# A two-block transformer in float32: new orders in the first stage, attention in head pairs, and the position products moved behind other projections

## The chip, the cores and the metric

One core of a Trainium2 chip runs the whole program. The time is device microseconds of one execution. TensorE is called PE here, VectorE DVE, ScalarE ACT, and SyncE SP; SP issues the loads.

## The reference, cut to what matters

256 tokens of width 2048 run through two blocks in float32.

```python
# first block: x, ctx are [256, 2048]
mod = silu(c) @ w_ada + b_ada                     # also for c_ctx; six vectors of 2048
h   = rms_norm(x) * (1 + sc_a) + sh_a             # the same for ctx with its own vectors
qa, kva, kr, cb, cc, ch = split(h @ w_in)         # ctx gives keys and values only
s   = q_nope @ k_nope.T + q_rope @ k_rope.T       # 8 heads: 128 + 64 wide, 256 + 256 keys
att = softmax(s / sqrt(192)) @ v
x   = x + gt_a * (rms_norm_by_group(concat(att, conv)) @ w_out)
x   = rms_norm(x + gt_f * conv_ffn(modulate(rms_norm(x))))       # 5504 wide
# second block, layers i = 0 (sparse attention) and 1 (stick-breaking attention)
x = layer_norm(ALPHA * x + (o * silu(gate)) @ w_o, g, b)
x = x + (p[i] @ w_ple[i]) * sigmoid(x @ w_ple_gate[i])           # p[i] is [256, 256]
```

## The kernel before, in words

Activations lie feature-major: a tile [128, k, 256] holds 128 features of block k for 256 tokens. A weight matrix comes in raw chunks of up to 1 MB on SP's queue into 4 slots (`issue`, L338). A unit of 1024 columns of a chunk is split in two: ACT casts a high part wh (L357), DVE subtracts for the low part wl (L358). A product is three matmuls of 256 columns, wh·xh, wl·xh, wh·xl (`mm3`), all recorded at L409. Splits run 4 units ahead of the matmuls (`look`, `unit`), with 5 buffers, and a chunk's slot is loaded anew when its last unit is split.

Tables fix the order. FIRST gives the matmul order of the first stage: `a` is a w_ada quarter, whose chunk PE takes raw, c and q the first columns of the short convolution and the query, k the keys and values. LOADS gives the order of their loads. LATE says after which chunk of a later weight a "late" block of w_ada follows, 64 in all: these are reduced on DVE, one instruction of 2048 columns each (L347), in the same queue as the splits. Work off the main product runs as generators in three lanes (EV, SIDE, MISC), which `pump` steps once after a unit.

First stage: four transposes give CBC; `gen_r0` sums the squares of x (w = 0) or ctx (w = 1) and multiplies by a matrix of ones; after each four `a`, `gen_h` writes SHG (shift and scale) and X, XH, XL for two blocks. Then come the short convolution's group 1, kv norm, the key and value products (wkvk, wkvv), the queries (wqb) with rope on KR and QR, and the rest of the convolution, between whose units `gen_att` runs one head and 128 queries at a time, up to four at once (ATT = (4, 2)).

w_out's first two groups end together (`turns`); then `resid` takes groups: it adds into x (`upd`, for w_out `upd_out`), squares, sums, and ends with matmuls with ones. PSUM has a ring of 2 tiles with 2 banks each (MR) and one of 4 banks (SR), so w_out's third group starts when `upd_out` has read the first.

At the end of each layer `finish_layer` runs w_o through `resid`, the four groups of p @ w_ple, the layer norm (`gen_ln`, `pair`), and the gate product. p arrives as PF, split in PH and PL.

## Time and profile before

| | us |
|---|---|
| three runs | 2202.58, 2196.92, 2197.62 (median 2197.62) |
| the profiled execution, its own time | 2194.55 |
| its span | 2192.7 |
| PE busy | 2148.4 (98%) |
| DVE busy | 1494.7 (68%) |
| ACT busy | 1104.9 (50%) |

Times in the rows are in the span's microseconds. In a timeline a row has its start, its duration (from the first start to the last end for a row with xN), the engine, the line, the operation, out<-in with shapes, and in brackets how long the engine was idle before it and who released it. In the list of waits "A <- B" says that A's engine waited for B. PEclk is the clock granted to PE, 1.00 being 2.4 GHz and 0.50 being 1.2 GHz. A matmul on 32-bit data that are not split (ones, scores) shows as two records.

### The profile page before, as it was taken

The numbers are of one execution on the slowest core, as the hardware profiler recorded it, in microseconds if no ns is written. First come the engines' busy times: TensorE is split into PE (matmuls) and PEld (weight loads), VectorE is DVE, ScalarE is ACT, GpSimd is POOL, SyncE is SP. The second block draws the span as 40 slices with busy tenths as digits, with TensorE's granted clock in tenths as the row PEclk, the third lists the DMA queues.
The fourth block names the chain that finished last, engine by engine and source line by source line (L and its number), as shares of the span: only waits on it lengthen the run. The fifth ranks groups of instructions, "written<-read, shape, count | busy, mean of one in ns | idle before, by whom it ended". The sixth has DMA issues, their size and how long they took to land.

```text
span 2192.7 us, 40082 instructions
## 1 busy us (share of the span) xinstructions
PE 2148.4 (98%) x17272; PEld 2058.8 (94%) x17272; DVE 1494.7 (68%) x1992; ACT 1104.9 (50%) x1512; POOL 0.2 (0%) x4
## 2 busy tenths in 40 slices
PE   5999999999999999999999999999999999999999
PEld 3779789989999999999999999999999999999999
DVE  4457878878767676757877669666666746646575
ACT  4345455445544444445656443445446546645363
POOL 0000000000000000000000000000000000000000
PEclk9999999999999999999999999999999999999999
DMA  9874878867666666645555544444555554455553
GB/s 395 335 278 175 324 260 308 344 242 288 230 223 239 231 233 236 223 176 190 187 187 187 186 164 177 150 154 154 197 174 181 188 192 142 147 173 190 181 176 113
DMA packets 68434, 467.71 MB, mean 213 GB/s; under 512 B 7840, under 2 KB 8352, under 8 KB 16544
## 3 DMA queue, kind: packets, MB, share of 16 engines
q1 hardware_dynamic: 68256, 465.14, 58.6%
q8 instruction: 135, 2.21, 0.4%
q14 instruction: 43, 0.35, 0.0%
HBM read 463.01 MB, written 2.10 MB: 212 GB/s over the span
## 4 chain that ended last, share of the span: by engine, by line
PE 94%; DMA 2%; DVE 2%; ACT 1%; issue 0%; SPq 0%; DVEq 0%; ACTq 0%
PE m L409 80%; PE s L409 14%; DMA raw<-in_wada 1%; DMA rawx<-in_wqa 1%; PE s L406 1%; DVE wl L358 1%; ACT wh L357 0%; DMA X<-in_xt 0%; DVE sq L616 0%; DVE raw L347 0%; DVE rp L1285 0%; DVE rp L1286 0%; DVE X L1144 0%; ACT uf L1204 0%; DVE uf L1212 0%
## 5 line engine op out<-in xcount | busy, mean ns | idle before, releaser
L409 PE MATMUL m<-XH,wh 128*128 128x256 f32 x4032 | 1144.8, 284 | 5.8 <-ACT XH L1185 4.1
L358 DVE TENSOR_TENSOR wl<-raw,wh 128x1024 fp32r<-128x1024 f32 (+1 forms) x672 | 800.2, 1197 | 502.9 <-ACT wh L357 501.6
L409 PE MATMUL m<-XH,wl 128*128 128x256 f32 x4032 | 1133.2, 281 | 2.9 <-DVE wl L358 2.9
L409 PE MATMUL m<-XL,wh 128*128 128x256 f32 x4032 | 1133.2, 281 | 0.3 <-DVE XL L1188 0.3
L357 ACT CAST wh<-raw 128x1024 fp32r<-128x1024 f32 (+1 forms) x672 | 687.0, 1029 | 665.8 <-PE m L409 587.4
L409 PEld LDWEIGHTS m<-XH,wh 128*128 128x128 f32 x4032 | 762.7, 189 | 27.6 <-issue 20.7
L409 PEld LDWEIGHTS m<-XH,wl 128*128 128x128 f32 x4032 | 762.5, 189 | 6.4 <-DVE wl L358 3.3
L409 PEld LDWEIGHTS m<-XL,wh 128*128 128x128 f32 x4032 | 762.2, 189 | 0.7 <-DVE XL L1188 0.6
L409 PE MATMUL m<-ahl,wh 128*128 128x256 f32 x1376 | 245.0, 281 | 0.5 <-DVE uf L1213 0.5
L409 PEld LDWEIGHTS m<-ahl,wh 128*128 128x128 f32 x1376 | 211.3, 188 | 0.7 <-issue 0.7
L409 PE MATMUL m<-ahl,wl 128*128 128x256 f32 x688 | 193.1, 281 | 0.0
L347 DVE SCALAR_TENSOR_TENSOR raw<-raw,CBC 128x2048 f32<-128x2048 f32 x64 | 145.0, 2283 | 0.0
L409 PEld LDWEIGHTS m<-ahl,wl 128*128 128x128 f32 x688 | 129.7, 189 | 0.0
L409 PE MATMUL s<-XH,wh 128*128 128x256 f32 x416 | 117.9, 283 | 7.1 <-ACT XH L649 7.1
L409 PE MATMUL s<-XL,wh 128*128 128x256 f32 x416 | 117.9, 283 | 0.0
L409 PE MATMUL s<-XH,wl 128*128 128x256 f32 x416 | 117.6, 283 | 0.0
L362 ACT CAST ahl<-AC 128x512 fp32r<-128x512 f32 x88 | 53.7, 610 | 89.0 <-PE m L409 89.0
L409 PEld LDWEIGHTS s<-XH,wh 128*128 128x128 f32 x416 | 79.4, 191 | 7.3 <-ACT XH L649 7.3
L363 DVE TENSOR_TENSOR ahl<-AC,ahl 128x512 fp32r<-128x512 f32 x88 | 59.6, 677 | 38.5 <-ACT ahl L362 38.5
L409 PEld LDWEIGHTS s<-XH,wl 128*128 128x128 f32 x416 | 79.4, 191 | 0.0
L409 PEld LDWEIGHTS s<-XL,wh 128*128 128x128 f32 x416 | 79.4, 191 | 0.0
L358 DVE TENSOR_TENSOR wl<-rawx,wh 128x768 fp32r<-128x768 f32 (+1 forms) x24 | 25.0, 1046 | 60.7 <-ACT wh L357 60.7
(387 smaller groups left out, 1683.4 us busy)
## 6 DMA issues: line engine op xcount, KB each, us to landing
raw<-in_wada SPq DMA_DIRECT2D x96, 1024.0 KB, 7.0
raw<-in_wup SPq DMA_DIRECT2D x86, 1024.0 KB, 4.9
raw<-in_wdown SPq DMA_DIRECT2D x40, 1024.0 KB, 4.8
raw<-in_wpg SPq DMA_DIRECT2D x32, 1024.0 KB, 4.9
raw<-in_wconv SPq DMA_DIRECT2D x28, 768.0 KB, 5.6
raw<-in_wout SPq DMA_DIRECT2D x16, 1024.0 KB, 6.4
raw<-in_wqA SPq DMA_DIRECT2D x16, 1024.0 KB, 4.8
raw<-in_wgA SPq DMA_DIRECT2D x16, 1024.0 KB, 4.8
```

The costliest lines, as they stand in the source:

```text
L347: V.scalar_tensor_tensor(r, r, 1.0, CBC, op0=OP.mult, op1=OP.mult, accum_out=ADA[:, b:b + 1])
L357: S.copy(e.wh[:, :n], r)
L358: V.tensor_tensor(e.wl[:, :n], r, e.wh[:, :n].bitcast(F32), OP.subtract)
L362: S.copy(e.x[:, 0, :e.nk], a)
L363: V.tensor_tensor(e.x[:, 1, :e.nk], a, e.x[:, 0, :e.nk].bitcast(F32), OP.subtract)
L406: count[0] = TE.transpose(o, i, ident)
L409: count[0] = TE.matmul(ps, l, r, start=start, stop=stop, skip_group_check=True, **kw)
```

## The change

1. LOADS: C0 moves between the second and third `a`; in the steady part each Q goes behind the two `a` that it preceded. After every fourth `a`, `look(1)` becomes `look(0)`. CBC is copied by DVE, not ACT. The sums for x are started before the first `a`, their ones matmul comes behind the second; those for ctx run at one go behind c1, with 8 matmuls with ones in place of most of the adds.
2. LATE: the convolution gets 24 blocks instead of 30, wkvv 1 and wqb 5 that had none.
3. `gen_att` takes two heads at a time, two such pairs at once (ATT = (2, 4)); the two 64-row products stand side by side, one on rows 0 to 63, the other on rows 64 to 127.
4. The layers' output projections end in two halves of 256 columns, as w_out did. In `resid` the sums of the first half go into `acc` on DVE, and only the last two blocks are summed by matmuls at the end. `ones` holds 1/2048 from w_out on.
5. Of the 8 groups of p @ w_ple, 2 go behind w_out, 3 behind the first w_o and 3 behind the second (before: 0, 4, 4). Early results are parked in DRAM (stored on ACT's queue, loaded on SP's). `parts`, which loads pf and splits it, now stands ahead of `resid`.

The rows in the following lists are in program order of one engine.

PE at the first scores, before (KN, QN: 128-wide part; KR, QR: 64-wide part):

```order
1049 L409 MATMUL m<-XL,wh 128x256
1050 L409 MATMUL s<-KN,QN 128x512
1051 L409 MATMUL s<-KR,QR 128x512
1052 L409 MATMUL m<-XH,wh 128x256
1053 L409 MATMUL m<-XH,wl 128x256
1054 L409 MATMUL m<-XL,wh 128x256
```

PE at the same place, after:

```order
1052 L415 MATMUL m<-XL,wh 128x256
1053 L415 MATMUL s<-KN,QN 128x512 x2
1054 L415 MATMUL s<-KR,QR 128x512 x2
1055 L415 MATMUL m<-XH,wh 128x256
1056 L415 MATMUL m<-XH,wl 128x256
1057 L415 MATMUL m<-XL,wh 128x256
```

Two heads' 128-wide products now stand together, and then their two 64-wide ones.

DVE in the middle of w_out, before (gta: the gate vector; X<-m,gta,X: `upd_out`; raw,ADA: a late block):

```order
310 L347 SCALAR_TENSOR_TENSOR raw,ADA<-raw,CBC 128x2048 x2
311 L358 TENSOR_TENSOR wl<-raw,wh 128x1024 x4
312 L1141 TENSOR_TENSOR gta<-ADA,vecs 128x16
313 L1144 SCALAR_TENSOR_TENSOR X<-m,gta,X 128x256 x4
314 L347 SCALAR_TENSOR_TENSOR raw,ADA<-raw,CBC 128x2048 x2
315 L358 TENSOR_TENSOR wl<-raw,wh 128x1024
316 L1144 SCALAR_TENSOR_TENSOR X<-m,gta,X 128x256 x4
```

DVE at the same place, after (ph<-pf,ph: the subtraction in `parts`):

```order
291 L353 SCALAR_TENSOR_TENSOR raw,ADA<-raw,CBC 128x2048 x2
292 L364 TENSOR_TENSOR wl<-raw,wh 128x1024 x4
293 L1213 TENSOR_TENSOR gta<-ADA,vecs 128x16
294 L1218 MEMSET ones 128x128
295 L1062 TENSOR_TENSOR ph<-pf,ph 128x512
296 L1216 SCALAR_TENSOR_TENSOR X<-m,gta,X 128x256 x4
297 L353 SCALAR_TENSOR_TENSOR raw,ADA<-raw,CBC 128x2048 x2
298 L364 TENSOR_TENSOR wl<-raw,wh 128x1024
```

The subtraction, which needs pf from DRAM and ACT's cast of it, now stands ahead of `upd_out`.

DVE from the query norm to the query products, before (QAL: the queries' low part; rp, KR: rope on the keys):

```order
128 L358 TENSOR_TENSOR wl<-raw,wh 128x1024
129 L550 TENSOR_TENSOR X<-X 128x256
130 L551 SCALAR_TENSOR_TENSOR X<-X 128x256
131 L552 SCALAR_TENSOR_TENSOR X<-X 128x256
132 L827 SCALAR_TENSOR_TENSOR X<-X,vecs 128x256 x4
133 L830 TENSOR_TENSOR QAL<-X,QAH 128x1024
134 L358 TENSOR_TENSOR wl<-raw,wh 128x1024 x2
135 L780 STREAM_SHUFFLE rp<-KR 128x256
136 L781 TENSOR_TENSOR rp<-rp,cst_1118 128x256
137 L782 TENSOR_TENSOR KR<-KR,cst_1118 128x256
138 L783 TENSOR_TENSOR KR<-KR,rp 128x256
139 L358 TENSOR_TENSOR wl<-raw,wh 128x1024 x3
```

DVE over the same stretch, after:

```order
133 L364 TENSOR_TENSOR wl<-raw,wh 128x1024
134 L353 SCALAR_TENSOR_TENSOR raw,ADA<-raw,CBC 128x2048 x2
135 L364 TENSOR_TENSOR wl<-raw,wh 128x1024
136 L802 STREAM_SHUFFLE rp<-KR 128x256
137 L803 TENSOR_TENSOR rp<-rp,cst_1125 128x256
138 L804 TENSOR_TENSOR KR<-KR,cst_1125 128x256
139 L805 TENSOR_TENSOR KR<-KR,rp 128x256
140 L364 TENSOR_TENSOR wl<-raw,wh 128x1024
141 L353 SCALAR_TENSOR_TENSOR raw,ADA<-raw,CBC 128x2048 x2
142 L364 TENSOR_TENSOR wl<-raw,wh 128x1024 x2
143 L353 SCALAR_TENSOR_TENSOR raw,ADA<-raw,CBC 128x2048
144 L364 TENSOR_TENSOR wl<-raw,wh 128x768
```

Five late blocks now stand between the splits of wqb and of the convolution.

```diff
 FIRST = "aaaacq" "aaaac" "aaakakqc" + 5 * "aaaakqc" + "kq"
-LOADS = "aaaaCQ" "aaaaK" + 3 * "aaaaCaaKQaa"
+LOADS = "aaCaaQ" "aaaaK" + 3 * "aaaaCaaKaaQ"
...
-ATT = (4, 2)
+ATT = (2, 4)
 LATE = {
-    "wconv": {0: 2, 5: 1, 7: 2, 8: 1, 9: 2, 10: 2, 11: 2, 12: 1, 13: 2, 14: 1, 15: 1, 16: 1, 17: 3, 20: 2, 21: 2,
-              22: 1, 23: 1, 24: 3},
+    "wconv": {2: 1, 3: 1, 5: 1, 7: 1, 8: 1, 9: 1, 10: 1, 11: 1, 12: 1, 13: 1, 14: 1, 15: 1, 16: 1, 17: 2, 20: 2,
+              21: 2, 22: 1, 23: 1, 24: 3},
     "wkvk": {0: 1},
+    "wkvv": {0: 1},
+    "wqb": {0: 2, 1: 2, 2: 1},
...
         "wgA": (KD, [512] * 4),
-        "woA": (KD, [512] * 4),
+        "woA": (KD, [512] * 3 + [256] * 2),
...
     }
...
     spec = _specs()
...
     plan_with_late("wout", [0, 4, 1, 5, 2, 6, 3, 7] + list(range(8, 16)))
+    plan("wple0", [0])
...
         c = list(range(len(lay[n])))
-        plan(n, three + c[12:] if n in ("wpg0", "wpg1") else c)
+        plan(n, three + c[12:] if n in ("wpg0", "wpg1") else c[1:] if n in ("wple0", "wple1") else c)
+        if n == "wple0":
+            plan("wple1", [0])
...
         yield
         yield from newton(dst, m)
-    def newton(dst, m):
-        S.activation(dst, m, AF.Ln)
+    def rstd_mean(dst, src):
+        m = cp.tile([P, T], F32, name="rsm", tag="rsm")
+        S.activation(dst, src, AF.Ln, bias=eps[:, 0:1])
+        V.tensor_scalar(m, src, EPS, None, op0=OP.add)
+        yield from newton(dst, m, False)
+    def newton(dst, m, log=True):
+        if log:
+            S.activation(dst, m, AF.Ln)
...
                 acc = sq
-            V.tensor_tensor(acc[:, 0], acc[:, 0], acc[:, 1], OP.add)
-            yield
-            yield
-            mm(ps, ones, acc[:, 0], True, True)
+                if w and q % 2:
+                    for j in range(2):
+                        mm(ps, ones, sq[:, j], q + j == 1, q + j == 8)
+                    acc = None
+            if not w:
+                V.tensor_tensor(acc[:, 0], acc[:, 0], acc[:, 1], OP.add)
+                yield
+                mm(ps, ones, acc[:, 0], True, True)
             rstd(R0[:, w, :], ps, 1.0 / D, EPS)
             r0_done.add(w)
...
                 tr(b.t[:, k * P:(k + 1) * P], CF[:, 0, 4 * c + k:4 * c + k + 1].to_broadcast([P, P]))
-            S.copy(CBC[:, 512 * c:512 * c + 512], b.t)
-        for _ in gen_r0(0):
-            pass
+            V.tensor_copy(CBC[:, 512 * c:512 * c + 512], b.t)
+        r0 = gen_r0(0)
+        next(r0)
         def ada(i):
...
             done_with(u.chunk)
+            if i == 1:
+                next(r0, None)
...
             if kc == 3:
-                look(1)
+                look(0)
         kvb = [m0.t[:, 0], m0.t[:, 1], m1.t[:, 0]]
...
             else:
+                unit_b(n, 0, banks[n], xh, xl, (0, 2) if n == "q" else (0,))
                 if n + str(i) == "c1":
-                    EV.add(gen_r0(1))
-                    pump()
-                unit_b(n, 0, banks[n], xh, xl, (0, 2) if n == "q" else (0,))
+                    for _ in gen_r0(1):
+                        pass
...
                 pump()
         with tc.tile_pool(name="b1s", bufs=1) as bs:
-            W2 = Ring(lambda: bs.tile([P, 512], F32, name="w2", tag="w2", bufs=6), 6, pump)
-            def gen_att(h, q):
-                r0 = 64 * (h % 2)
+            W2 = Ring(lambda: bs.tile([P, 2, 512], F32, name="w2", tag="w2", bufs=3), 3, pump)
+            def gen_att(hp, q):
+                hs = (2 * hp, 2 * hp + 1)
                 qc = slice(q * P, (q + 1) * P)
-                s = yield from SR.get()
...
+                ss = []
+                for _ in hs:
+                    ss.append((yield from SR.get()))
+                for h, s in zip(hs, ss):
+                    mm(s.t, QN[:, h, qc], KN[:, h, :], True, False)
+                for e, s in enumerate(ss):
+                    r = slice(64 * e, 64 * e + 64)
+                    mm(s.t, QR[r, hp, qc], KR[r, :], False, True)
+                yield
+                sm = bs.tile([P, 4, 2], F32, name="sm1", tag="sm1", bufs=4)
+                for e, s in enumerate(ss):
+                    V.tensor_reduce(sm[:, 0, e:e + 1], s.t, axis=AX.X, op=OP.max)
+                V.tensor_scalar(sm[:, 1], sm[:, 0], -scale1, None, op0=OP.mult)
                 yield
                 p = yield from W2.get()
...
+                yield
+                pt = yield from W2.get()
+                for e in range(2):
+                    tb = yield from SR.get()
+                    for k in range(4):
+                        tr(tb.t[:, k * P:(k + 1) * P], p.t[:, e, k * P:(k + 1) * P])
+                    yield
+                    S.copy(pt.t[:, e], tb.t)
+                    tb.free()
                 p.free()
                 yield
...
         return
-    def resid(pool, name, xh_, xl_, upd, acc, fin=None, pre=None, first=(), into=None):
+    def ple(layer, g, ph, ahead):
+        m = Banks(SR.now(), SR.now()) if ple_at[0] == 0 else MR.now()
+        ple_at[0] += 1
+        unit_b(f"wple{layer}", g, lambda n: m.bank(n // 2)[:, n % 2 * T:(n % 2 + 1) * T],
+               lambda k, u: ph[:, 0, k, :], lambda k, u: ph[:, 1, k, :], ahead=ahead)
+        return m
...
+    def parts(pool, layer, tags):
+        pf = pool.tile([P, 2, T], F32, name="pf", tag=tags[0], bufs=tags[1])
+        ph = pool.tile([P, 2, 2, T], F32R, name="ph", tag=tags[2], bufs=tags[3])
+        nc.sync.dma_start(pf, A["pt"][layer])
+        S.copy(ph[:, 0], pf)
+        V.tensor_tensor(ph[:, 1], pf, ph[:, 0].bitcast(F32), OP.subtract)
+        return ph
+    ple_at = [0]
+    def resid(pool, name, xh_, xl_, upd, acc, fin=None, pre=None, first=(), into=None, fill=None,
+              sqe=None):
         n_acc = acc.shape[1]
...
+        halves = len(spec[name][1]) == 5
+        def fold():
+            V.tensor_tensor(acc[:, :, 0], acc[:, :, 0], acc[:, :, 1], OP.add)
+        def total():
+            b = yield from SR.get()
+            mm(b.t[:, :n_acc * T], ones, acc[:, :, 0], True, False)
+            tot.append(b)
         def gen(g, m):
             yield
...
                 fin(g)
-            if g == 2:
-                V.tensor_tensor(acc[:, :, 0], acc[:, :, 0], acc[:, :, 1], OP.add)
+            if g == 2 and not halves:
+                fold()
                 for _ in range(3):
                     yield
-                b = yield from SR.get()
-                mm(b.t[:, :n_acc * T], ones, acc[:, :, 0], True, False)
-                tot.append(b)
+                yield from total()
...
             pump()
...
             m.free()
-        def sums(ns):
...
+        def gen_end(m):
+            yield
+            end(m, (12, 13))
+            yield
+            V.tensor_tensor(acc[:, 0], acc[:, 0], sq[:, 0:2], OP.add)
+            if n_acc == 2:
+                V.tensor_tensor(acc[:, 1], acc[:, 1], X[:, 12:14, :], OP.add)
+            fold()
+            for _ in range(2):
+                yield
+            yield from total()
+        last = None if halves else group_b(name, 3, xh_, xl_)
+        sq = pool.tile([P, 4, T], F32, name="sqe", **sqe)
         if halves:
-            EV.add(gen_end(group_b(name, 3, xh_, xl_), (12, 13)))
+            EV.add(gen_end(group_b(name, 3, xh_, xl_)))
             pump()
             end(group_b(name, 4, xh_, xl_), (14, 15))
+            if n_acc == 2:
+                V.tensor_tensor(sq[:, 0], X[:, 14, :], X[:, 15, :], OP.add)
         else:
-            end(group_b(name, 3, xh_, xl_), range(12, 16))
+            end(last, range(12, 16))
...
             fin(3)
+        if fill:
+            fill()
         if into is not None:
...
-            sums((14, 15) if halves else range(12, 16))
+            if n_acc == 2:
+                mm(b.t[:, T:], ones, sq[:, 0], False, True)
+            for n in (14, 15):
+                mm(b.t[:, :T], ones, sq[:, n - 12], False, n == 15)
             return b
         return finish
...
         def upd_out(n, ps):
             V.scalar_tensor_tensor(X[:, n, :], ps, gta[:, n:n + 1], X[:, n, :], op0=OP.mult, op1=OP.add)
-        b = resid(b2, "wout", xh, xl, upd_out, acc, first=m_out)()
-        rstd(RF, b.t[:, :T], 1.0 / D, EPS)
+        V.memset(ones, 1.0 / D)
+        W4 = dict(tag="w4", bufs=4)
+        ph = parts(b2, 0, ("w4", 4, "w4", 4))
+        ple_out, ple_kept = [], dp.tile([P, 12, T], F32, name="plek")
+        def fill_out():
+            ple_at[0] = 0
+            ple_out.append(ple(0, 0, ph, 3))
+        b = resid(b2, "wout", xh, xl, upd_out, acc, first=m_out, fill=fill_out, sqe=W4)()
+        ple_out.append(ple(0, 1, ph, 2))
+        for _ in rstd_mean(RF, b.t[:, :T]):
+            pass
         b.free()
         def modulation(c):
...
                 V.tensor_tensor(XL[:, k, :], t[:, k, :], XH[:, k, :].bitcast(F32), OP.subtract)
             hf_done.add(0)
+        AC = b2.tile([P, NF, T], F32, name="AC")
         hf_first()
-        for _ in hf(1):
-            pass
-        AC = b2.tile([P, NF, T], F32, name="AC")
+        for g, m in enumerate(ple_out):
+            keep(AC[:, 4 * g:4 * g + 4, :], m)
+            nc.scalar.dma_start(ple_kept[:, 4 * g:4 * g + 4, :], AC[:, 4 * g:4 * g + 4, :])
+            if g == 0:
+                for _ in hf(1):
+                    pass
         def gen_up(g, m):
             ps = [m.bank(n // 2)[:, (n % 2) * T:(n % 2 + 1) * T] for n in range(4)]
...
     def finish_layer(pool, layer, wo, wp, wg, last):
-        PF = pool.tile([P, 2, T], F32, name="pf")
-        nc.sync.dma_start(PF, A["pt"][layer])
-        PH = pool.tile([P, 2, T], F32R, name="ph")
-        PL = pool.tile([P, 2, T], F32R, name="pl")
         acc = pool.tile([P, 2, 2, T], F32, name="accl")
         PW = pool.tile([P, KD, T], F32, name="PW")
+        jobs = ((1, 1), (1, 2), (1, 3)) if last else ((0, 2), (0, 3), (1, 0))
+        ph = {}
+        for n in dict.fromkeys(l for l, _ in jobs):
+            ph[n] = parts(pool, n, ("pf", 1, f"ph{n}", 1))
+        if last:
+            nc.sync.dma_start(PW[:, 0:4, :], ple_kept[:, 8:12, :])
+        else:
+            nc.sync.dma_start(PW[:, 0:8, :], ple_kept[:, 0:8, :])
         def upd(n, ps):
             V.scalar_tensor_tensor(X[:, n, :], X[:, n, :], ALPHA, ps, op0=OP.mult, op1=OP.add)
...
                 pin()
-                S.copy(PH, PF)
-                V.tensor_tensor(PL, PF, PH.bitcast(F32), OP.subtract)
-        finish = resid(pool, wo, xh, xl, upd, acc, fin)
+        out_banks = []
+        def fill(i=0):
+            n, g = jobs[i]
+            out_banks.append(ple(n, g, ph[n], 3 - i))
+        def store(i):
+            n, g = jobs[i]
+            if n == layer:
+                keep(PW[:, 4 * g:4 * g + 4, :], out_banks[i])
+            else:
+                t = pool.tile([P, 4, T], F32, name="pn")
+                keep(t, out_banks[i])
+                nc.scalar.dma_start(ple_kept[:, 8:12, :], t)
+        ple_at[0] = 0
+        tot = resid(pool, wo, xh, xl, upd, acc, fin, fill=fill)()
+        fill(1)
+        fill(2)
...
         rs = pool.tile([P, T], F32, name="rsl")
-        def gen_ln(tot):
...
+        ps = tot.t
+        V.tensor_copy(mu, ps[:, T:])
+        V.tensor_tensor(v, mu, mu, OP.mult)
+        V.tensor_tensor(v, ps[:, :T], v, OP.subtract)
+        V.tensor_scalar(v, v, 0.0, LN_EPS, op0=OP.max, op1=OP.add)
+        tot.free()
+        steps = newton(rs, v)
+        next(steps)
+        store(0)
+        next(steps, None)
+        V.tensor_tensor(mu, mu, rs, OP.mult)
+        store(1)
...
-        def ple(g):
...
+        first_pair()
+        both(pair(1))
+        store(2)
...
-        group_three(wg, pair, lambda g, m: EV.add(gen_ple(4 * g, 2, m)), (1, 0, 0))
+        group_three(wg, pair, lambda g, m: EV.add(gen_ple(4 * g, 2, m)), (0, 0, 1))
...
```

## Rows read from the trace of the kernel before

**Rows 1.** The page, chain of waits: shares of the span by engine.

```profile
PE 94%; DMA 2%; DVE 2%; ACT 1%; issue 0%; SPq 0%; DVEq 0%; ACTq 0%
```

**Rows 2.** Stretches: us, busy time (instructions) of PE, PEld, DVE, ACT, POOL; PEclk; DMA share; GB/s.

```profile
155.00:180.00 25.00, 22.67 (x153) 20.76 (x152) 20.69 (x26) 10.85 (x15) 0.00 (x0) 0.86 0.54 201
178.00:220.00 42.00, 42.00 (x262) 37.39 (x261) 32.81 (x48) 26.42 (x39) 0.00 (x0) 1.00 0.44 156
480.00:494.00 14.00, 9.41 (x57) 8.10 (x57) 6.85 (x18) 4.78 (x10) 0.00 (x0) 0.88 0.31 124
560.00:1545.00 985.00, 983.51 (x8152) 967.25 (x8151) 707.28 (x976) 495.15 (x673) 0.00 (x0) 1.00 0.56 196
```

**Rows 3.** Waits of PE over the whole run: total us, times, longest.

```profile
PE s L409 <- ACT XH L649: 7.1, 2, 5.1
PE s L409 <- DMA raw<-in_wada: 4.5, 5, 1.4
```

**Rows 4.** Timeline, all engines, around 26 us: start, duration, instruction, [idle before].

```profile
25.95 1.23 DVE L358 TENSOR_TENSOR wl<-rawx,wh 128x1024 fp32r<-128x1024 f32 x1 [1.70 <-ACT wh L357]
27.09 0.16 DVE L636 TENSOR_TENSOR SHG<-m,vecs 128x8 f32<-128x8 f32 x1
...
28.57 0.58 PE L409 MATMUL s<-XH,wh 128*128 128x256 f32 x1 [5.12 <-ACT XH L649]
```

**Rows 5.** Timeline, DVE and then PE, 155 to 161 us.

```profile
155.23 2.28 DVE L347 SCALAR_TENSOR_TENSOR raw<-raw,CBC 128x2048 f32<-128x2048 f32 x1
...
160.65 0.39 PE L409 MATMUL m<-XH,wl 128*128 128x256 f32 x1 [1.74 <-DVE wl L358]
```

**Rows 6.** Groups of PE by form, 217 to 425 us: busy us, mean ns.

```profile
L409 PE MATMUL s<-KR,QR 64*128 64x512 f32 x32 | 18.0, 641 | 0.0
```

**Rows 7.** Timeline of PE: a head's scores, and later the 64-row products of layer A.

```profile
220.59 1.12 PE L409 MATMUL s<-KR,QR 64*128 64x512 f32 x2
221.65 0.39 PE L409 MATMUL m<-XH,wh 128*128 128x256 f32 x1
...
1289.35 1.14 PE L409 MATMUL s<-CBC,IQ 64*128 64x256 f32 x8
1290.42 0.39 PE L409 MATMUL m<-XH,wh 128*128 128x256 f32 x1
```

**Rows 8.** Timeline, all engines, the middle of w_out.

```profile
435.31 0.33 SPq L338 DMA_DIRECT2D raw<-in_wout  x1
...
435.40 1.66 DVE L1144 SCALAR_TENSOR_TENSOR X<-m,gta,X 128x256 f32<-128x256 f32 x4
...
437.21 0.36 PE L409 MATMUL m<-XH,wh 128*128 128x256 f32 x1 [1.46 <-DVE X L1144]
```

**Rows 9.** DMA issues: count, KB each, median us from issue to landing.

```profile
pf<-in_pt SPq DMA_DIRECT2D x2, 256.0 KB, 3.2
...
KR<-in_pos SPq DMA_DIRECT2D x1, 128.0 KB, 5.9
```

**Rows 10.** Timeline, all engines, the end of w_out.

```profile
489.64 0.38 PE L409 MATMUL m<-XH,wh 128*128 128x256 f32 x1 [4.10 <-ACT XH L1185]
```

**Rows 11.** Timeline of PE and DVE, end of the first layer of the second block.

```profile
1631.13 0.28 PE L409 MATMUL m<-ph,wh 128*128 128x256 f32 x1
...
1633.93 0.59 PE L409 MATMUL s<-X,ones 128*128 128x256 f32 x2
...
1637.20 0.47 PE L409 MATMUL m<-ph,wh 128*128 128x256 f32 x1
...
1637.59 0.42 DVE L1358 TENSOR_SCALAR mu<-s 128x256 f32<-128x256 f32 x1 [1.07 <-PE s L409]
...
1641.92 0.69 DVE L1369 TENSOR_TENSOR X<-X,rsl 128x512 f32<-128x512 f32 x1
...
1645.15 0.69 DVE L1377 TENSOR_TENSOR XL<-X,XH 128x512 fp32r<-128x512 f32 x1 [0.49 <-ACT XH L1375]
...
1645.87 0.28 PE L409 MATMUL s<-XH,wh 128*128 128x256 f32 x1
```

More of the change, by code (lines that the diff above doesn't have):

```diff
@@ L106, in _specs, with _layout @@
     }
-def _layout(kt, groups):
+def _layout(kt, groups, single=False):
     chunks, cur, off = [], [], 0
@@ L414, in mm3, with unit_b @@
         mm(ps, wh, xl, False, stop)
-    def unit_b(name, g, pst, xh, xl, starts=(0, 2)):
-        u = unit(name, g)
+    def unit_b(name, g, pst, xh, xl, starts=(0, 2), ahead=None):
+        u = unit(name, g, ahead)
         kt = spec[name][0]
@@ L1262, in gen_rf @@
             yield
[L1263 removed]
+            yield from rstd_mean(RF, tot2.t[:, :T])
             tot2.free()
@@ L1354, in finish_layer, with first_pair @@
         rs = pool.tile([P, T], F32, name="rsl")
[L1356 to L1365 removed]
+        ps = tot.t
[10 more added lines that the diff above has]
+        store(1)
+        def first_pair():
+            for k in range(2):
+                x, g, b = X[:, k, :], vec(f"ln_g{layer}", k), vec(f"ln_b{layer}", k)
+                V.tensor_tensor(x, x, rs, OP.mult)
+                V.tensor_tensor(x, x, mu, OP.subtract)
+                S.activation(XH[:, k, :], x, AF.Identity, scale=g, bias=b)
+            for k in range(2):
+                x, g, b = X[:, k, :], vec(f"ln_g{layer}", k), vec(f"ln_b{layer}", k)
+                V.tensor_scalar(x, x, g, b, op0=OP.mult, op1=OP.add)
+                V.tensor_tensor(XL[:, k, :], x, XH[:, k, :].bitcast(F32), OP.subtract)
         def pair(q):
```

94 lines of the change are left out of this document (29 added, 65 removed).

## The prediction

> **What bounds the kernel now.** I read the chain of waits first: PE has 94% of it [rows 1]. So the time is what PE does, plus the places where it stands or runs slowly, and work on another engine counts only where PE waits for it. The table of stretches says where those places are: from 560 to 1545 us PE is idle for 1.5 us of 985 [rows 2], while the stretches of the first stage and the ends of w_out have idle time or a clock under 1.00 [rows 2]. The list of waits names who ends them [rows 3], and the timeline gives each its place. Durations are of the profiled execution, 2194.55 us; the median of the runs, 2197.62, stands 3.07 above it, and I add that at the end.
>
> **First loads and steady loads.** PE waits 5.12 us until 28.57 for its first XH; SHG, from which XH comes, is ready to be written but stands on DVE behind a split that begins at 25.95 only because Q0 has landed, and itself starts at 27.09 [rows 4]. With `look(0)` that split no longer stands ahead, which frees at least 1.23 us, its duration. Against it, C0 in front of the third `a` delays that chunk by a load of 768 KB, and the sums for ctx, now in one go behind c1, put their DVE work ahead of k0's split. In the steady part PE waits 4.5 us for w_ada chunks in 5 pieces [rows 3]; Q's going behind them takes part of it, but Q itself then comes later. Between a gain of both waits' larger part (4 us) and a loss of 2 us I take -1.5.
>
> **The convolution's first group.** Two late blocks of 2.28 us stand ahead of four splits on DVE, and PE waits 1.74 us until 160.65 [rows 5]. In the 25 us around it PE is idle for 2.33, and a clock of 0.86 costs another 25 x 0.14 = 3.5, so 5.8 is the most that can be had [rows 2]. The change moves both blocks back by two and three chunks. What is late next is the chain of the kv norm, which needs the last of ctx's keys and then ACT and DVE by turns; it stays where it is. I take -3.2, with 0 and -5.8 as ends.
>
> **Late blocks between the key products and the first scores.** One wkvv block and five wqb blocks come into a stretch in which PE never stops: 6 x 2.28 = 13.7 us, where DVE has 42.00 - 32.81 = 9.2 us idle [rows 2, 5]. So DVE ends this stretch some 4.5 us later, and the order puts blocks in pairs between the splits of wqb and of the next weights; the looked-ahead units cover two units or so of PE. If DVE's gaps and the look-ahead take it all, the cost is 0; if all of the 13.7 - 9.2 shows and a pair stalls one split as in rows 5 and its clock follows, 8. I take +5, near the excess of 4.5, since the stretch has no idle time on PE to hide it.
>
> **Head pairs.** 16 products with 64 rows stand as 32 records [rows 6]. One takes 221.65 - 220.59 = 1.06 us, 17.0 in all; in layer A four products of 256 columns on alternate halves of the rows, the same columns as a pair of these, take 1290.42 - 1289.35 = 1.07 [rows 7]. Eight pairs so cost 8.6: -8.4. If the two halves ran one after the other it would be 0. The rest of the attention's matmuls is unchanged in number.
>
> The Trainium skill (TensorE: Matmul & The Clock Gate, Part 3: Packing small matmuls) says that matmuls on different rows overlap from their start within about 4 ns, but start and end strictly in program order. If a 32-bit product's two passes had to end before its neighbour's, three passes would be left of four and the pair would save about 4 us in all instead of 8.4. Rows 7 agree with full overlap.
>
> **pf ahead of w_out's first additions.** Now DVE begins `upd_out` at 435.40, four of them take 1.66, and PE, which needs the bank, goes on at 437.21 after 1.46 us [rows 8]. After the change the subtraction in `parts` stands ahead, and it waits for pf, issued on SP behind a raw chunk of 435.31. Landing takes 3.2 us as for pf in the layers, with free engines, or 5.9 as for the loading of positions behind a raw chunk [rows 9]. ACT's cast and DVE's subtraction of 512 columns add 0.69 each, as the same size does in rows 11, then 1.66 and 0.15 to PE's start. PE thus goes on at 435.64 + 3.2 + 1.38 + 1.81 = 442.0, or at 444.7: +4.8 to +7.5. Behind the waiting subtraction on DVE stand `upd_out`, two late blocks and the next splits; the look-ahead has those ready for PE. Because a load stands directly ahead I take 7.3. PE's clock may fall after so long a stop: the 4.10 us at the end of w_out [rows 10] are followed by 14 x 0.12 = 1.7 us lost [rows 2]. With a part of that, +8 (5 to 10).
>
> By the Trainium skill (DMA: Bandwidth & Descriptors, Anatomy of one DMA) a transfer costs a fixed 2.0 us and its bytes at 436 GB/s: 2.6 us for pf alone, as an estimate, and PE would go on at 441.4, +4.2. Rows 9 have 3.2 for it where nothing stands ahead, and the measurement decides.
>
> **The end of w_out.** Two groups of p @ w_ple come in. A group takes 1633.93 - 1631.13 = 2.80 us [rows 11], so +5.6. They stand in the wait of 4.10 [rows 10]: one in front of the last sums, one behind them. The chain from the sums to XH is as long as that wait, so the second covers 2.8 of it and about 1.5 stays: -2.6. Two matmuls with ones fewer, at (1637.20 - 1633.93) / 8 = 0.41, make -0.8, and a shorter stop may keep the clock: -1.4 of the 1.7. Sum +0.8; -1.5 if all is hidden, +3 if neither wait nor clock gets better.
>
> **The ends of the layers.** From the last w_o matmul to the gate's first, PE has 1645.87 - 1631.13 = 14.74 us of work without a gap: four groups of 2.80 and eight sums of 0.41 [rows 11]. After: three groups and three sums, 9.6. That is less cover for the layer norm. From the sums to its factors it takes 1641.92 - 1637.59 = 4.33, and to the first pair's XL another 3.92 (1645.15 + 0.69 - 1641.92) with the second pair's work between [rows 11]. The new `first_pair` has half as wide instructions; I take 2.8, so XL is there 7.1 after the sums, while two groups of products last 5.6: a wait of 1.5. The second pair, no longer interleaved, comes at most 4.33 + 2 x 3.92 = 12.2 after the sums; at about 11.5 against one unit of 2.8 begun at 7.1 that is a wait of 1.6. So 9.6 + 3.1 = 12.7, and -2.0 a layer, -4.0 in all. If nothing waits it is -10; if the chain takes the full 3.92 per pair, 0.
>
> **Sum.** -1.5 - 3.2 + 5 - 8.4 + 8 + 0.8 - 4.0 = -3.3: 2194.55 - 3.3 = 2191.3 as a profiled execution, 2194.3 on the runs' scale.
>
> **Rivals.** *The stops stay covered (faster).* DVE is idle for a third of the run; if its queue takes the six late blocks in its gaps, pf lands in 3.2 us and the layer norm's second pair is not waited for, the terms become 0, +5 and -6: 10 us less, 2184. For it speaks that splits run 4 units ahead; against it that PE has no slack in the stretch of the late blocks [rows 2].
> *A lagging DVE holds up each pair (slower).* A pair's maximum stands on DVE behind late blocks and splits. Before, three other heads were in flight; now one other pair, and all of its four SR banks are taken by the scores of two pairs. If a pair's transposes come late by one late block, 2.28 us, eight times, that is +18: about 2212. It decides once DVE's lag exceeds the four steps between scores and transposes, three units of convolution or so. For it speaks that the lag of 4.5 us begins just before the first pair; against it that the convolution carries six late blocks fewer.
> *The pairs don't run side by side.* Then -8.4 goes and the time is 2203. Rows 7 speak against it.
>
> **How the numbers follow.** The forecast has 0.40, the faster case 0.38, the lagging DVE 0.17, pairs without overlap 0.05. About 0.3%, 6.6 us, is what can be told from no change: faster is under 2191.0, slower above 2204.2. The forecast's own terms spread by some 5 us, so a fifth of it falls below and a twentieth above; the faster case is nearly all below. That gives 0.43 faster, 0.37 same, 0.20 slower. The range reaches from below the faster case to short of the lagging one: 2179 to 2208; the forecast's own is 2187 to 2202.
>
> **What would show it.** Right: PE's largest wait in w_out's middle ends with X from `upd_out` and behind it the subtraction of pf, 5 us or more; 64-row records of two heads start within some ns of each other; no stop at the convolution's first group, but waits on wl between 195 and 225 us; each layer's gate begins about 12.7 us behind w_o, with a wait on XL. Wrong: no wait at pf, waits on the transposes, or a gate that starts without a gap.

## The result, and the profile after

The changed kernel takes 2228.4 us in the median of 4 runs (2223.96 to 2230.32); the kernel before took 2197.27 beside it. The ratio is 1.0135, 95% interval 1.0121 to 1.0149: 31 us slower. The forecast was 2194.3, 3 us faster, in a range of 2179 to 2208, and the slowest of its rivals stood at 2212. The profiled execution took 2223.96, its span is 2222.2.

The chain of waits on the page after, against [rows 1]: PE has 5 points less; DVE has 3 more, and DMA, ACT and issue 1 each (rounded).

```profile
PE 89%; DVE 5%; DMA 3%; ACT 2%; issue 1%; SPq 0%; ACTq 0%; DVEq 0%
```

The list of PE's waits over the whole run after, its first rows, against [rows 3] (total us, times, longest):

```profile
PE m L415 <- ACT wh L363: 10.8, 4, 3.1
PE m L415 <- DVE X L1216: 9.8, 1, 9.8
PE s L415 <- DMA raw<-in_wada: 8.7, 4, 5.5
PE s L415 <- ACT XH L669: 4.0, 2, 2.0
PE m L415 <- ACT arow L649: 3.7, 4, 1.5
...
PE m L415 <- DVE wl L364: 3.0, 4, 0.9
PE m L415 <- ACT QR L902: 2.8, 1, 2.8
PE s L412 <- ACT w L944: 2.5, 1, 2.5
```

New are the second row, the pf stop that was forecast, and the first: splits that come too late, which were not (one in the first stage, one at the start of the first layer's output projection, one at the end of each layer). In the three stretches with the stops in w_out and in the first layer, in the columns of [rows 2], the mean granted clock is 0.66, 0.85 and 0.90, a mixture of its two levels 0.50 and 1.00:

```profile
430.00:445.00 15.00, 5.18 (x34) 5.01 (x33) 7.32 (x11) 2.83 (x4) 0.00 (x0) 0.66 0.47 185
1552.00:1575.00 23.00, 20.10 (x145) 19.59 (x144) 12.35 (x14) 9.33 (x13) 0.00 (x0) 0.85 0.50 182
1645.00:1680.00 35.00, 30.40 (x216) 28.65 (x216) 23.11 (x37) 17.59 (x27) 0.00 (x0) 0.90 0.42 151
```

The first of these stretches in the kernel before, at 1.00 and with 116 matmuls instead of 34:

```profile
430.00:445.00 15.00, 13.54 (x116) 13.37 (x115) 12.91 (x18) 5.14 (x6) 0.00 (x0) 1.00 0.99 396
```

The middle of w_out after, in order of time, against [rows 8]: pf is issued at 431.54, ACT's cast starts 6.8 us later, and PE goes on at 441.41 after 9.82 us instead of 1.46.

```profile
431.54 0.38 SPq L1060 DMA_DIRECT2D pf<-in_pt  x1
438.35 0.62 ACT L1061 CAST ph<-pf 128x512 fp32r<-128x512 f32 x1 [8.52 <-DMA pf<-in_pt]
...
439.00 0.69 DVE L1062 TENSOR_TENSOR ph<-pf,ph 128x512 fp32r<-128x512 f32 x1 [7.68 <-ACT ph L1061]
439.61 1.65 DVE L1216 SCALAR_TENSOR_TENSOR X<-m,gta,X 128x256 f32<-128x256 f32 x4
...
441.41 0.55 PE L415 MATMUL m<-XH,wh 128*128 128x256 f32 x1 [9.82 <-DVE X L1216]
```

The start of the first layer's output projection after. Two parts of p go through one pf buffer, so the second load waits for the first subtraction; ACT is held until 1566.5, and PE, out of split weights, stops for 2.22 and 0.68 us.

```profile
1559.31 4.29 SPq L1060 DMA_DIRECT2D pf<-in_pt  x2
...
1561.90 0.62 ACT L1061 CAST ph<-pf 128x512 fp32r<-128x512 f32 x1 [3.35 <-DMA pf<-in_pt]
...
1565.87 0.62 ACT L1061 CAST ph<-pf 128x512 fp32r<-128x512 f32 x1 [3.35 <-DMA pf<-in_pt]
...
1567.49 0.58 PE L415 MATMUL m<-XH,wh 128*128 128x256 f32 x1 [2.22 <-ACT wh L363]
...
1568.75 0.58 PE L415 MATMUL m<-XH,wl 128*128 128x256 f32 x1 [0.68 <-DVE wl L364]
```

The end of the same layer after, against [rows 11]. The first XH comes in time, almost (0.32). But the casts of the gate's next units stand behind the whole layer norm and the parking of a result (pn) on ACT, and start at 1668.87; PE stops for 2.99 us and then 0.68. At the end of the second layer it stops in the same way, for 2.5 and 0.9 us.

```profile
1662.71 0.38 PE L415 MATMUL m<-XH,wh 128*128 128x256 f32 x1 [0.32 <-ACT XH L1482]
...
1667.40 1.06 ACT L1053 COPY pn<-m 128x512 f32<-128x512 f32 x2
...
1668.87 4.83 ACT L363 CAST wh<-raw 128x1024 fp32r<-128x1024 f32 x5 [0.40 <-ACT pn L1053]
...
1669.96 0.58 PE L415 MATMUL m<-XH,wh 128*128 128x256 f32 x1 [2.99 <-ACT wh L363]
...
1671.22 0.58 PE L415 MATMUL m<-XH,wl 128*128 128x256 f32 x1 [0.68 <-DVE wl L364]
```

These stops don't make 31 us: by the two pages PE is idle for 44.3 us before (2192.7 - 2148.4) and for 61.1 after (2222.2 - 2161.1), 16.8 more, and busy for 12.7 more. This is how the difference of the two profiled executions grows (us from the span's start; the last column is for the run with all mends, at the end of the experiments):

| | before | after | after less before | all mends |
|---|---|---|---|---|
| first product of the keys | 177.87 | 175.43 | -2.4 | 175.62 |
| first scores | 219.64 | 221.58 | +1.9 | 224.77 |
| last matmul on dg (the norm by group, ahead of w_out) | 412.84 | 408.43 | -4.4 | 406.40 |
| first product of w_up | 489.64 | 496.71 | +7.1 | 484.34 |
| end of the first layer's output projection | 1631.13 | 1651.67 | +20.5 | 1626.47 |
| end | 2192.7 | 2222.2 | +29.5 | 2185.5 |

The largest step, 13.5 us, lies between w_up and the end of the first layer's output projection, where PE has only 2.9 us of new waits. The stretches 600 to 640 us (in w_up) and 1585 to 1625 us (a layer's output projection) are full in both kernels, at clock 1.00, but hold different numbers of matmuls. First before (341 instead of 343 because two longer products with ones stand at its end):

```profile
600.00:640.00 40.00, 40.00 (x343) 40.00 (x342) 28.36 (x35) 18.45 (x25) 0.00 (x0) 1.00 0.65 233
1585.00:1625.00 40.00, 40.00 (x341) 39.83 (x340) 25.13 (x31) 16.99 (x19) 0.00 (x0) 1.00 0.53 185
```

And after:

```profile
600.00:640.00 40.00, 40.00 (x339) 40.00 (x339) 26.98 (x33) 19.47 (x25) 0.00 (x0) 1.00 0.69 240
1585.00:1625.00 40.00, 40.00 (x335) 40.00 (x335) 23.59 (x31) 18.08 (x19) 0.00 (x0) 1.00 0.53 181
```

From start to start of neighbouring 256-column products the distance is 117.3 ns, 118.7 ns or 120.0 ns, and a stage keeps one of these, called levels here, for hundreds of products (343 in 40 us are the first level, 339 the second, 335 the third; a count takes in those that overlap the edges). One level over 14,000 products is 14,000 x 1.33 ns = 19 us. Summed over all steady products, from start to start, the trace before lies about 9.5 us above the lowest level and the trace after about 19.7; which products count as steady moves such a sum by 1 to 2 us.

### The profile page after: what moved, and what is told of

Same layout as the page of the kernel before. It is cut to its first block, busy times and chain, and to the rows that moved or that the text cites. A ratio compares the mean times of both kernels' runs of the same rounds, so it can differ in the third digit from the quotient of the medians.

```text
span 2222.2 us, 40078 instructions
## 1 busy us (share of the span) xinstructions
PE 2161.1 (97%) x17258; PEld 2075.0 (93%) x17262; DVE 1499.5 (67%) x1997; ACT 1102.0 (50%) x1508; POOL 0.2 (0%) x4
## 4 chain that ended last, share of the span: by engine, by line
PE 89%; DVE 5%; DMA 3%; ACT 2%; issue 1%; SPq 0%; ACTq 0%; DVEq 0%
PE m L415 75%; PE s L415 13%; DVE wl L364 2%; DMA rawx<-in_wqa 1%; DMA raw<-in_wada 1%; DVE raw L353 1%; PE s L412 1%; DMA pf<-in_pt 1%; ACT wh L363 0%; DMA raw<-in_wconv 0%; DMA X<-in_xt 0%; DVE rp L1373 0%; DVE rp L1374 0%; ACT arow L649 0%; ACT X L1494 0%
## 5 line engine op out<-in xcount | busy, mean ns | idle before, releaser
L415 PE MATMUL s<-XL,wh 128*128 128x256 f32 x416 | 118.7, 285 | 0.0
```

What stands on the lines that cost most here:

```text
L415: count[0] = TE.matmul(ps, l, r, start=start, stop=stop, skip_group_check=True, **kw)
```

## The experiments

The theory after these traces: a good half of the loss is stops of PE (pf in w_out, pf in the first layer, late splits behind each layer norm) with the clock that they cost, the rest is the spacing. The rivals differ on what sets the spacing.

**The kernel before again (no edit).**

> The kernel before, run once more. In the two traces so far the distance from one 256-column product to the next has one of three levels, 117.3, 118.7 or 120.0 ns, that hold for whole stages: before has 117.3 in w_up and 118.7 in the first three groups of w_down, the changed kernel has them the other way round. If the level is drawn anew in each execution (at the stop that precedes the stage), this trace has other levels in some stages than the first, and its time lies up to 10 us off 2194.55. If the level belongs to the program, every stage has the level that it had, and the time is within 3 us.

2200.49 us in its one profiled run, against a median of 2194.24 for the 8 runs beside it. w_up now has the second level, w_down and the projections have those they had:

```profile
600.00:640.00 40.00, 40.00 (x339) 40.00 (x338) 27.23 (x34) 18.62 (x23) 0.00 (x0) 1.00 0.65 221
1585.00:1625.00 40.00, 40.00 (x343) 40.00 (x342) 24.75 (x31) 17.35 (x19) 0.00 (x0) 1.00 0.53 185
```

So the same program can have another level for w_up in another execution. That makes about 5.7 us between the two traces, and part of the scatter of a few us between the runs.

**The kernel before, moved by 32 bytes, and by 64.** A tile of 4 bytes a row, as the change has it, moves what is declared behind it by 32 bytes; the second run has `[P, 9]` in its place, 36 bytes, which moves it by 64. X, XH and XL are declared ahead of it and stay.

```diff
     ones = cp.tile([P, P], F32, name="ones")
+    eps = cp.tile([P, 1], F32, name="eps")
...
         V.memset(ones, 1.0)
+        V.memset(eps, EPS)
```

> The kernel before with one 4-byte tile more in the constants' pool, set once and not read, as the changed kernel has it: all later tiles, the split weights among them, lie 32 bytes further on. Theory 1 (the level follows from where operands lie): w_up goes to 118.7 ns, w_down's first groups to 117.3, and the time rises by about 4 to 10 us. Theory 2 (the level follows from the instructions and their timing): levels and time as before, within 3 us.

> The kernel before with a spare tile of 36 bytes, which moves later tiles by 64 bytes instead of 32. Theory 1a (how the weights lie to a step of 64 bytes, relative to XH and XL, matters): as the kernel before, 2194 to 2200, w_o's projections at 117.3 ns. Theory 1b (any move off the old places costs): as the shift by 32, 2207 to 2213, w_o's projections at 120.0 ns.

By 32 bytes: 2209.01 against 2194.24, ratio 1.0065 (1.0045 to 1.0084): 10 to 18 us, more than the 4 to 10 that I expected. w_up has the second level, the first layer's output projection the third, as in the changed kernel:

```profile
600.00:640.00 40.00, 40.00 (x339) 40.00 (x339) 26.80 (x31) 18.97 (x24) 0.00 (x0) 1.00 0.66 232
1585.00:1625.00 40.00, 40.00 (x335) 40.00 (x335) 22.23 (x27) 16.76 (x18) 0.00 (x0) 1.00 0.54 185
```

w_down's first groups stayed at 118.7, where I expected 117.3: that one differs by more than the place. By 64 bytes: 2220.18 against 2197.65, ratio 1.0106 (1.0088 to 1.0124), all four runs within 1.7 us; this too is more than either theory had. Now w_up too is at the third level, and only w_down is at the first:

```profile
600.00:640.00 40.00, 40.00 (x336) 40.00 (x335) 25.77 (x30) 19.41 (x24) 0.00 (x0) 1.00 0.65 231
1585.00:1625.00 40.00, 40.00 (x335) 40.00 (x335) 22.86 (x28) 17.77 (x19) 0.00 (x0) 1.00 0.53 185
```

Theory 1a, a step of 64 bytes, is refuted; moving the tiles costs at either step. Nothing else in these kernels changed but a tile that DVE sets once and nobody reads.

The traces of all runs together, those of the later experiments too, show what follows the place and what doesn't (ns from product to product, and in how many traces):

| tiles | w_up | w_down, first groups | first layer's output projection |
|---|---|---|---|
| in place, 9 traces | 117.3 in 7, 118.7 in 2 | 118.7 in 8, 117.3 in 1 | 117.3 in 9 |
| moved by 32 bytes, 4 traces | 118.7 in 4 | 117.3 in 2, 118.7 in 1, 120.0 in 1 | 120.0 in 3, 118.7 in 1 |
| moved by 64 bytes, 1 trace | 120.0 | 117.3 | 120.0 |

The projection's level parts the places cleanly; w_down's does not follow the place.

**The changed kernel with eps out of the way.**

```diff
-    VE = cp.tile([P, NVEC], F32, name="vecs")
+    VE = cp.tile([P, NVEC + 1], F32, name="vecs")
+    eps = VE[:, NVEC:NVEC + 1]
...
-    eps = cp.tile([P, 1], F32, name="eps")
...
```

> The changed kernel with its 4-byte tile eps held in spare bytes at the end of the vectors' tile, so that the split weights lie where they lay before; nothing else. Theory 1 (part of the level follows from where operands lie): the two output projections of the layers, at 120.0 ns in the changed kernel and 117.3 before, go back to 117.3 or at most 118.7, and the time falls by 5 to 10 us, to 2218 to 2223. Theory 2 (it is the order and the stops that set the level): projections stay at 120.0 and the time within 3 us of 2228.

2212.38 us, ratio to before 1.0075 (1.0061 to 1.0090): 13 us less than the changed kernel by the ratios, 16 by the medians, where 5 to 10 were expected. The two stretches are back at the first level:

```profile
600.00:640.00 40.00, 40.00 (x343) 40.00 (x342) 26.78 (x32) 19.23 (x24) 0.00 (x0) 1.00 0.69 238
1585.00:1625.00 40.00, 40.00 (x343) 40.00 (x343) 23.20 (x29) 16.39 (x17) 0.00 (x0) 1.00 0.50 180
```

Steady products lie about 7.7 us above the lowest level here, 12 less than in the changed kernel's trace. The stops are all there still.

**pf split later in w_out, and then in the layers, with more look-ahead.** Both keep eps where the change put it. With `True` as its last argument `parts` only loads pf; ACT's cast and DVE's subtraction come behind the first group's sums.

```diff
-        ph = parts(b2, 0, ("w4", 4, "w4", 4))
+        ph = parts(b2, 0, ("w4", 4, "w4", 4), True)
...
```

> The changed kernel, but in w_out pf is only loaded ahead of the additions; ACT's cast and DVE's subtraction come behind the first group's sums. Theory of the stops: PE's wait of 9.8 us at 431 to 441 becomes about 1.5, as before, and with the clock that stays up the time falls by 8 to 10 us, to 2219. Rival (the wait is covered by slack later, or the transfer is late in any case): under 3 us less. Levels of the spacing may move the time by another 5 us either way.

2217.07 us, ratio to before 1.0096 (1.0072 to 1.0120): 8.6 us less than the change by the ratios, as expected, though its four runs spread over 10 us. The traces agree: from the last matmul on dg to w_out's first sums with ones it is 79.87 us in the changed kernel (408.43 to 488.30) and 70.23 here (408.67 to 478.90), 9.6 less. The wait is what it was before:

```profile
433.26 0.36 PE L415 MATMUL m<-XH,wh 128*128 128x256 f32 x1 [1.43 <-DVE X L1229]
```

```diff
-            ph[n] = parts(pool, n, ("pf", 1, f"ph{n}", 1))
+            ph[n] = parts(pool, n, (f"pf{n}", 1, f"ph{n}", 1), True)
...
+            split_todo(g)
...
-            out_banks.append(ple(n, g, ph[n], 3 - i))
+            out_banks.append(ple(n, g, ph[n], None))
...
```

Here each part of p has a pf of its own, and `None` leaves the look-ahead at its full 4 units.

> As the run before, and in both layers too: each p has a buffer of its own and is split behind the first group's sums of w_o; and the p @ w_ple products look 4 units ahead instead of 3, 2 and 1, so that splits of the gate's weights come ahead of the layer norm on ACT and DVE. Theory of the stops: the 2.2 and 0.7 us waits at 1565 with their slow clock go (about -6), and the 3.0 and 0.7 us waits on splits behind each layer norm go with theirs (about -4 each): some 14 us less than the run before, 2205. Rival: the splits now delay the layer norm on DVE and ACT by as much as they gain, and only the 6 us remain: 2213.

2207.19 us, ratio to before 1.0056 (1.0038 to 1.0075): 9 to 10 us less again, not 14. In its trace the waits on splits at the layers are gone, and per layer 1.2 us on XH and under 1 on XL are left; but its steady products lie about 24.6 us above the lowest level, 6 more than in the run before (w_down has 120.0), which is about the difference.

**The parts of the first stage and the attention, each alone on the kernel before.**

Head pairs (`gen_att` and ATT as in the change):

> The kernel before with the head pairs alone (two heads at a time, at most two pairs at once); loads, late blocks and all else as before. Prediction's term: 64-row products side by side, 8.4 us less from the first scores to the end of the convolution, about 2186 against 2194. Rival (the pair itself makes its transposes wait, not the late blocks): PE waits 2 us and more on the transposes of the first pairs here too, and the gain is 3 to 6 us.

2194.34 against 2196.62, ratio 0.9986 (0.9975 to 0.9996): 3 us less (0.9 to 5.5). The products do stand side by side (below), but PE now waits for the probabilities once before the transposes, and twice, before products with V, for ACT's copy of the transposes; w is the tile of both:

```profile
PE s L406 <- ACT w L922: 3.1, 1, 3.1
...
PE s L409 <- ACT w L930: 2.1, 2, 1.2
```

8.4 - 5.2 = 3.2 fits: here the rival is right that pairs alone, without a late block moved, are waited for.

Late blocks (the new LATE):

> The kernel before with the new places of the late blocks alone. Prediction's terms: the stop at the convolution's first group goes (-3.2), and six blocks more between the key products and the first scores cost 5: +2 in all, with waits of PE in the query products (2 to 3 us) as in the changed kernel. Rival (the stops there come from the first stage's new orders): no such waits, and 3 us less than before.

2198.41, ratio 1.0013 (1.0003 to 1.0023), +2.9 by the ratio (0.7 to 5.1), as expected. The trace has the wait on QR:

```profile
PE m L411 <- ACT QR L882: 2.9, 1, 2.9
```

Up to the key products it is 3.0 us ahead of before (first product at 174.89 against 177.87), at the first scores 1.5 behind. The wait on QR has its own history, which the changed kernel's trace shows too: a chunk of wqb is issued only at 204.02, when DVE is done with a late block in one of the slots for raw chunks (before, all of wqb was issued by 181.6); ACT is idle for 8.63 us until it lands, its copy of QR stands behind the casts, and PE needs the bank that this copy frees.

```profile
204.02 0.33 SPq L344 DMA_DIRECT2D raw<-in_wqb  x1
...
210.78 1.99 ACT L363 CAST wh<-raw 128x1024 fp32r<-128x1024 f32 x2 [8.63 <-DMA raw<-in_wqb]
...
212.68 1.00 ACT L902 COPY QR<-m 128x1024 f32<-128x1024 f32 x1
...
213.74 0.38 PE L415 MATMUL m<-QAH,wh 128*128 128x256 f32 x1 [2.81 <-ACT QR L902]
```

First stage:

> The kernel before with the first stage's new orders alone (loads, look-ahead after each fourth quarter of w_ada, the sums of squares, the copies of CBC). Prediction's term: -1.5. From the changed kernel's trace: waits of 5.5 us for the first chunk and 3.1 us on k's first split replace those of 7.7, 5.1 and 2.5; the first stage ends within 1.5 us of before, so the time is within 3 us. Rival (a gain hidden by the late blocks): 4 us less.

2199.38, ratio 1.0014 (1.0001 to 1.0027): +3 (0.2 to 5.9). The waits moved:

```profile
PE s L409 <- DMA raw<-in_wada: 8.1, 4, 5.0
PE m L409 <- ACT arow L633: 4.3, 4, 1.4
...
PE s L409 <- ACT XH L653: 3.5, 2, 2.0
...
PE m L409 <- ACT wh L357: 3.1, 1, 3.1
```

XH's wait is half of that in [rows 3], and the one for the squares of x, 10.2 us before, is 0.6; in their place PE waits 5.0 us for w_ada's first chunk, 2.0 for the third, which now comes behind C0, and 3.1 for k's first split, and the waits on arow (ACT's copies of w_ada's products) have gone from 1.5 to 4.3. The first XH is not earlier for it: 28.43 against 28.57. The loads are what is full here: DMA's share of the first 60 us is 0.94 in both kernels, which fits that a wait that goes comes back at the next chunk. The last product with w_ada is 0.2 us later than before and the first key product 1.4. One pair of traces can't place 3 us here: in the seven traces with the old first stage the last product on arow starts between 139.4 and 143.3 us, in the seven with the new one between 141.2 and 144.8 (means 141.0 and 142.6).

**All mends together.** The changed kernel with both edits on pf, the look-ahead and eps in spare bytes; then also with the old LATE; then also with the old first stage.

> The changed kernel with all three mends: pf split behind the first group's sums in w_out and in the layers, 4 units of look-ahead through the p @ w_ple products, and eps in spare bytes so that the split weights lie as before. Theory (stops plus spacing): from the 2212 of the run with eps moved, 8 us for the stop in w_out, 6 for the one in the first layer and 4 to 8 for the gate's splits go: 2190 to 2196, at or below the kernel before. Rival (the mends in part undo each other, or levels are drawn anew): 2200 or more.

2191.76, ratio 0.9972 (0.9958 to 0.9986). Its levels are about 7.9 us above the lowest, and of PE's waits those of the first stage, 3.3 us on QR and small ones, 1.5 us at most, are left:

```profile
600.00:640.00 40.00, 40.00 (x343) 40.00 (x343) 29.39 (x37) 19.30 (x24) 0.00 (x0) 1.00 0.67 234
1585.00:1625.00 40.00, 40.00 (x343) 40.00 (x343) 25.84 (x33) 17.95 (x21) 0.00 (x0) 1.00 0.49 171
```

> The same with the old places of the late blocks (30 in the convolution, none behind wkvv and wqb). The new places alone gave +1.8 (interval 0.7 to 5.1) on the kernel before; so 2 us less than the run before is expected, with PE's wait of 3 us on QR gone and the stop at the convolution's first group back. Rival (with pairs the convolution's late blocks hold up the transposes): 3 us more.

2189.99, ratio 0.9975 (0.9961 to 0.9989): the same by the ratios, 1.8 us less by the medians, where 2 were expected. Eight of its 12 runs lie between 2187.5 and 2190.9, three between 2197.7 and 2198.6, one between; the profiled one, 2198.57, has the second level in w_up.

> The same as the run before with the old orders of the first stage as well: what is left of the change is the head pairs, the moved p @ w_ple products, the halves and the sums on VectorE. The first stage's orders alone gave +2.8 (interval 0.2 to 5.9), so about 2 us less again: 2186 to 2192, the fastest of all, some 5 us under the kernel before. Rival: the two parts depend on each other and the time is as the run before or more.

2189.03, ratio 0.9967 (0.9953 to 0.9981): the fastest median, 8.6 us under before, though not told apart from the two others. What remains of the change in it is the head pairs, the moved products, the halves and the sums.

## Why the prediction was wrong

The forecast had the sign of five of its seven terms. It failed in one term, the ends of the layers, and in two steps that were no terms at all: the time of a product, and pf in the layers.

- **PE's rate.** The sum took the time of a product as given and counted instructions and waits. The change moved every tile behind eps by 32 bytes, and PE's spacing went up by one level in w_up and by two in the first layer's output projection (in w_down it fell by one). Putting the tiles back gave 13 to 16 us; moving the kernel before by as much cost it 14 to 15. This is nearly half of the loss. No row of before could have shown the price, but the levels were there to be seen: w_up (117.3 ns) and w_down (118.7) differ within it.
- **The ends of the layers, term -4.0.** The step that failed is "a wait of 1.6" for the second pair as the only cost of less cover besides the first pair's 1.5. The matmuls did shrink: from the end of the last w_o product (1651.67) to the gate's first at 1662.71 it is 11.0 us instead of 14.7. But I did not ask what stood behind the layer norm on ACT: with a look-ahead of 3, 2, 1 units the gate's next splits do, and cost 2.99 + 0.68 us, and with the clock at 0.90 over 35 us about another 3.5. That is some +3.5 a layer, not -2. With the look-ahead open, 1.3 and 0.4 us of waits remain, less than the 3.1 that I took, and from w_o to the gate it is 12.0 us (1626.47 to 1638.47): with this mend the term comes out near its forecast of 12.7.
- **pf in the layers, not priced.** I priced the pf load in w_out and let those in the layers pass, since the second block loads pf early before. In the first layer there are two, through one buffer: 2.9 us of waits, and 23 x (1 - 0.85) = 3.5 us by the clock, some 6 us.
- **pf in w_out, +8: right.** The wait rose by 8.4 us; landing took 6.8 against the 5.9 of [rows 9]. Undoing it gave 8.6 by the ratios and 9.6 between the traces. The 2.6 us that the prediction sets beside it by the Trainium skill (DMA: Bandwidth & Descriptors, Anatomy of one DMA) is a fit which that section gives for transfers that GpSimd issues; SP issues pf, which landed in 2.5 to 2.6 us in the layers of the changed kernel and in 6.8 here, behind raw chunks.
- **Late blocks, -3.2 and +5: sizes right, the second in part by luck.** Measured alone -3.0 to the key products, and +4.5 from there to the first scores. But the +5 was worked out from DVE falling behind, with waits of PE on wl between 195 and 225 us. The wait that came is on QR, at the end of a late load: a late block holds its slot until DVE has reduced it, and the chunk of wqb behind it comes 8.6 us late for ACT. That path was not in the prediction.
- **Head pairs, -8.4: right for the products, half right alone.** The products of the first pair stand as forecast, two in the time of one. PE after, four records for two products, then the next product:

```profile
223.39 1.13 PE L415 MATMUL s<-KR,QR 64*128 64x512 f32 x4
...
224.45 0.38 PE L415 MATMUL m<-XH,wh 128*128 128x256 f32 x1
```

  That is 1.06 for two against 1.06 for one in [rows 7]. The rule in the Trainium skill (TensorE: Matmul & The Clock Gate, Part 3) that products on different rows overlap holds here in full; no loss from their order shows. Alone the pairs gave 3 us, since 5.2 us of waits on the probabilities and their transposes came with them. In the changed kernel one such wait is left, 2.5 us, in place of the rival's eight; there the first pair's maxima do start late on DVE (230.46, behind a late block, for scores that end at 224.5), as the lagging-DVE rival says. With all mends there is none, and the stretch from the first scores to the last matmul on dg is 11.6 us shorter than before, first before and then with all mends:

```profile
219.64:412.84 193.20, 193.20 (x1391) 168.14 (x1390) 158.82 (x223) 102.72 (x195) 0.00 (x0) 0.99 0.84 306
224.77:406.40 181.63, 181.63 (x1391) 164.87 (x1390) 146.13 (x199) 100.22 (x187) 0.00 (x0) 1.00 0.80 294
```

  So in these traces the waits on the pairs go with the places of the late blocks: with the old places (the last two runs) 4.5 and 4.7 us of them are back. Why, no run shows, and the times of these runs are not told apart.
- **First stage, -1.5: wrong sign,** +3 alone. The gain at the first XH, from which the term came, did not come at all (28.43 against 28.57), and k's split behind ctx's work is waited for 3.1 us; I took the losses as smaller than the gain.
- **The end of w_out, +0.8: close.** From w_out's last product to w_up's first it was 6.4 us and is 8.4 (1.32 of it a wait), with less clock lost (0.97 instead of 0.91 over 480 to 500 us, 1.2 us).

```profile
496.71 0.39 PE L415 MATMUL m<-XH,wh 128*128 128x256 f32 x1 [1.32 <-ACT XH L1268]
```

The account in us, from runs: the places in memory 13 to 16, pf in w_out 8.6, pf and the late splits in the layers 9 to 10 (with the levels of that run against it). Together 31 to 35; with all three mended at once the changed kernel fell by 36, to 5.9 under before. So what the change was made of, without its three accidents, is a gain of 6 us (3 to 9 by the interval). The sum without the 8 for pf was -11.3, so about half of it came. The gains that the traces show are the pairs and the shorter ends of the layers. The first stage and the late blocks cost 3 each when put alone into the kernel before; taking them back from the mended kernel gave nothing that can be told from the scatter (ratios 0.9972, 0.9975, 0.9967).

What stays open: by what a place in memory sets the spacing, why w_up and w_down have more than one level at the same place while the first layer's output projection keeps 117.3 in all nine traces in place, and which tile's place counts; weights, raw chunks and all stage tiles were moved together, while X, XH and XL stayed.

## What to carry to other kernels

Where PE is full for hundreds of microseconds, compare the number of matmuls in equal stretches before any wait: one per cent of this run is 22 us, more than any stop here, and a 4-byte tile in front of the weight buffers can bring more than half of that. For every wait put into a queue, list what the queue holds behind it and how far the look-ahead reaches; here ACT's queue decided three times, though ACT is busy for only half of the run. And measure the parts of a change alone, and once more together: the parts that gained were hidden by one displaced tile and a few small stops, and the pairs were waited for longer alone than with the late blocks moved.

## What the runs showed of the hardware

- Steady products of 256 columns at a granted clock of 1.00 have one of three spacings, 117.3, 118.7 or 120.0 ns, mostly kept over a whole stage. The same program can have another one in another execution (w_up 117.3 and 118.7).
- Moving the tiles behind the constants by 32 bytes cost 15 us of 2194 (10 to 18), by 64 bytes 23 us of 2198 (19 to 27). Not every stage follows the place: w_down's first groups had 117.3 ns with the tiles moved by 64 bytes, all three levels when moved by 32, and 118.7 or 117.3 in place.
- Two 64-row products of 512 columns on different halves of the rows take 1.06 us together, as long as one.
- A load of 256 KB on SP's queue landed in 2.5 to 2.6 us in the changed kernel's layers, and in 6.8 us in w_out, where raw chunks had been issued right ahead of it.
